# Twelve pairs of gate tiles by seven products, attention pipelined and moved ahead of the convolution, eight modulation columns moved to the down projection

## The chip, the cores and the metric

The kernel runs on one core of a Trainium2 chip. The metric is the device time of one execution, in microseconds (us); several runs are taken and their median is compared. The profile is one execution taken by the hardware profiler, with times counted from its first instruction. Engines are named TensorE (PE in the profile; its weight loads are PEld), VectorE (DVE), ScalarE (ACT), GpSimd (POOL) and SyncE (SP), whose queue issues most of the transfers.

## The reference

One layer of a hybrid diffusion backbone, on 640 tokens: 512 of a sample (a grid 8 by 64) and 128 of a prompt. Everything is float32; the matmuls meet the accuracy by splitting each operand in a high and a low part and adding three products (high x high, high x low, low x high).

```python
def token_mixers(h, lw, ...):
    proj = h @ lw['w_in']
    (a_x, a_b, a_c, b_q, b_ff, b_fb, b_i, b_g, c_q, c_k, c_v, d_u, d_v) = jnp.split(proj, IN_SPLITS, axis=-1)
    y_a = a_b * dwconv3(a_c * a_x, lw['conv_a_w'], lw['conv_a_b'])
    y_b, s_f, s_b = hgrn2_bidir(b_q, b_ff, b_fb, b_i, b_g, ...)
    y_c = ...   # neighbourhood attention (sample), full attention (prompt)
    y_d = chunk_gmlp(d_u, d_v, lw['gmlp_norm_g'], lw['gmlp_ws'], lw['gmlp_b'])
    g_a, g_b, g_c, g_d = jnp.split(jax.nn.sigmoid(h @ lw['w_gate'] + lw['b_gate']), N_BRANCH, axis=-1)
    merged = (g_a * (y_a @ lw['w_br_a']) + g_b * (y_b @ lw['w_br_b'])
              + g_c * (y_c @ lw['w_br_c']) + g_d * (y_d @ lw['w_br_d']))
    return merged @ lw['w_o'], kh, vh, s_f, s_b

def trunk_layer(x, cvec, lw, ...):
    mod = jax.nn.silu(cvec) @ lw['w_ada'] + lw['b_ada']
    sh1, sc1, g1, sh2, sc2, g2 = jnp.split(mod, 6, axis=-1)
    h = rmsnorm(x, lw['norm1_g']) * (1.0 + sc1) + sh1
    mix, ... = token_mixers(h, lw, ...)
    x = x + g1 * mix
    h = rmsnorm(x, lw['norm2_g']) * (1.0 + sc2) + sh2
    x = x + g2 * conv_ffn(h, lw['w_up'], lw['ffn_conv_w'], lw['ffn_conv_b'], lw['w_down'])
```

The model width is 1024, each branch is 256 wide, the gates are 4 x 1024 columns, the feed-forward is 2 x 2816 up and 2816 down.

## The kernel before

The order of the large matmuls is written as a list of units (`units`). After the first part (norm, modulation columns 0 to 15 by matmul, and the first three tiles of the input projection) the units run in this order:

- **Input projection** in thirteen sections of two tiles (`SECTIONS`), h @ w_in. Most are `in_tile`: 128 output features by 640 tokens, 48 matmuls of 128x128 by 320 columns (8 k-steps, three products, two halves of 320 tokens). Sections i and dv are `tok_tile` (tokens on the partitions). `evac_in` takes each tile out of PSUM (pool `psg`, two buffers of two banks).
- **Gates** (`gate_tile`): for branches in the order a, d, b, c, each with 8 tiles of 128 columns. The plain form has 48 matmuls for the gate and 12 for the branch product y @ w_br; ScalarE takes the sigmoid, VectorE multiplies and adds into `merged` (regions MG0, MG1). Branches b and c are computed in `GPAIR` = 8 pairs of tiles (n, n + 4): `g_pair` computes the 2 x 2 block product of a pair with seven block products of 12 matmuls each (`gprod`, L1110) in place of eight, and two branch products of 12 (`g_branch`, L1123). For this it needs sums of weight blocks (`g_sums`) and four new operands from h (`g_operands`, from a copy of h in DRAM, `hdr`), which lie in regions that attention uses (X0, X1, F) and are computed once attention is done.
- **Output projection** (`wo_tile`), norm 2, **up projection** (`up_all`, 22 pairs by seven products), **down projection** (`down_tile`, two halves of 512 columns, 11 steps each, 30 matmuls a step; `down_out` multiplies by g2 and adds the residual).

Beside this stream run generators ("jobs"): `hgrn` (started at the end of section q), `gmlp` (du), `conva` (ab), `attn` (cv), `ada_cols` (q), `g_operands`. Each yields a time, and is taken on by `tick` when the estimated time of the matmuls traced so far (`now`) has passed it; that sets where its matmuls stand between the others. `SLACK` stretches a job's yields, `HD` holds yields. `drain` runs all jobs until a condition holds. The framework then orders each engine's instructions by this order and by what is ready in its own estimate; from the pairs on parts are kept in program order (`Ordered`).

`hgrn` runs seven levels on VectorE with small matmuls between (L533), state updates (L582), and, once section g is done, its outputs (L620 to L627) and transposes (L642). Its helper `along` (L476) multiplies ten blocks by two columns of ones, twice. At its end it splits y_b (region E) and y_d (region D) in high and low parts (`split_y`, L657). `attn` waits for y_d. It works on 16 units (8 windows x 2 heads) in four groups (`GS`); before each group it waits until another gate's sigmoid is traced (`R["sig"]`), then runs scores and exponentials for the group's four units (`s1`), then normalisation and transposes (`s2`, L847) and the value products (`s3`, L864). Its result, yc, is in region C.

`ada_cols` computes the modulation columns 16 to 47, each a 512 KB load into the one buffer H and two VectorE passes over 1024 elements (L248); columns 16 to 23 give g1, 24 to 39 give sh2 and sc2, 40 to 47 give g2. `gain_rows` transposes g1 or g2 and writes it to DRAM (`growd`), `gain_load` reads it back to all partitions (L271).

## Time and profile before

| | |
|---|---|
| median of 3 runs | 1061.43 us (1060.1, 1061.43, 1061.75) |
| profiled execution | 1065.27 us, span 1063.5 us |
| granted TensorE clock, mean | 0.989 |
| PE busy | 1038.6 us (98%), 7696 matmuls |
| DVE busy | 775.0 us (73%) |
| ACT busy | 517.3 us (49%) |
| POOL busy | 118.0 us (11%) |
| bytes moved | 155.05 MB |

A row of a timeline or of the chain gives its start, its length, the engine, the line and the operation, with the tiles written and read; x is the count merged into the row. Merged matmuls overlap, so the distance between the starts of two rows says more than a row's length. A row of stretches gives busy times by engine, the granted clock and the DMA load of each stretch.

### The profile page before, as it was taken

Reading aid. Unit: us, or ns where it says so; the run is one execution under the profiler, and the core shown is the slowest. Engines: PE = TensorE matmul, PEld = TensorE weight load, DVE = VectorE, ACT = ScalarE, POOL = GpSimd, SP = SyncE. Lnnn points to the kernel's source line nnn. Section 1 sums busy time; section 2 is a strip of 40 time slices with the busy share of each in tenths; the row PEclk is TensorE's granted clock in tenths of the full one; section 3 lists DMA queues with packets and bytes.
Section 4 is the critical chain, followed back from the end, with each engine's and each line's share of the span. In section 5 each row is a group of like instructions: output and inputs, shape, how many; then the busy total and the mean of one; then the engine's idle time right before and its main releaser. Section 6 shows DMA issues by size and latency. Waiting matters only on the chain.

```text
span 1063.5 us, 18801 instructions
## 1 busy us (share of the span) xinstructions
PE 1038.6 (98%) x7696; PEld 974.0 (92%) x7696; DVE 775.0 (73%) x1232; ACT 517.3 (49%) x863; POOL 118.0 (11%) x150
## 2 busy tenths in 40 slices
PE   7999999999999999999999998999999999999997
PEld 5699989999999999999998788999999999888886
DVE  6558898853688887676764687998888887745534
ACT  6252253332444422444452387777777667534432
POOL 1013120020011000000010022211221111001101
PEclk9998999999999999999999999999999999999999
DMA  9662334343443452212244258775566667952212
GB/s 373 229 215 88 121 101 139 123 126 112 131 149 110 160 162 85 86 53 97 89 140 159 100 160 167 176 184 144 144 154 163 163 165 208 371 189 78 80 40 100
DMA packets 53431, 155.05 MB, mean 146 GB/s; under 512 B 7745, under 2 KB 16353, under 8 KB 51681
## 3 DMA queue, kind: packets, MB, share of 16 engines
q1 hardware_dynamic: 42128, 130.11, 36.5%
q0 software_dynamic: 11216, 23.74, 10.9%
q8 instruction: 60, 0.98, 0.4%
q14 instruction: 27, 0.21, 0.1%
HBM read 124.44 MB, written 15.49 MB: 132 GB/s over the span
## 4 chain that ended last, share of the span: by engine, by line
PE 86%; DVE 7%; ACT 2%; DMA 2%; issue 2%; POOL 0%; SPq 0%; POOLq 0%; DVEq 0%; ACTq 0%
PE g L382 22%; PE g L1406 20%; PE m L1110 9%; PE g L1714 8%; PE m L1714 6%; PE m L1406 5%; PE g L1123 3%; PE m L1243 2%; PE g L1243 1%; PE g L926 1%; PE g L1816 1%; PE m L213 1%; DVE junk L248 1%; PE m L864 1%; DMA MG<-raw 1%
## 5 line engine op out<-in xcount | busy, mean ns | idle before, releaser
L382 PE MATMUL g<-XH,w 128*128 128x320 f32 x1088 | 258.0, 315 | 0.2
L382 PEld LDWEIGHTS g<-XH,w 128*128 128x128 f32 x1088 | 185.1, 188 | 4.9 <-issue 2.9
L382 PE MATMUL g<-XL,w 128*128 128x320 f32 x544 | 168.2, 309 | 0.0
L382 PEld LDWEIGHTS g<-XL,w 128*128 128x128 f32 x544 | 102.4, 188 | 0.3 <-issue 0.3
L348 DVE TENSOR_TENSOR w<-raw,w 128x1024 fp32r<-128x1024 f32 (+1 forms) x37 | 49.9, 1349 | 24.2 <-ACT w L347 23.5
L248 DVE SCALAR_TENSOR_TENSOR junk<-H,S 128x1024 bf16<-128x1024 f32 x32 | 41.2, 1288 | 19.5 <-DMA H<-in_w_adt_dram 19.4
L335 DVE TENSOR_TENSOR w<-raw,w 128x1024 fp32r<-128x1024 f32 x34 | 44.3, 1302 | 13.5 <-ACT w L334 12.2
L347 ACT ACTIVATE w<-raw 128x1024 fp32r<-128x1024 f32 (+1 forms) x37 | 42.6, 1152 | 20.4 <-PE g L382 10.0
L334 ACT ACTIVATE w<-raw 128x1024 fp32r<-128x1024 f32 x34 | 35.8, 1054 | 31.2 <-PE g L1243 15.8
L1714 PE MATMUL g<-w,XH 128*128 128x512 f32 (+1 forms) x216 | 47.5, 372 | 0.0
L1714 PEld LDWEIGHTS g<-w,XH 128*128 128x128 f32 x216 | 38.5, 188 | 7.3 <-DVE X L133 0.2
L133 DVE SCALAR_TENSOR_TENSOR X<-X,p2t,X 128x641 f32<-128x641 f32 x44 | 38.9, 884 | 2.4 <-ACT X L133 1.5
L133 DVE SCALAR_TENSOR_TENSOR X<-MG,p2t,X 128x641 f32<-128x641 f32 x44 | 38.9, 884 | 2.1 <-ACT X L133 1.2
L248 DVE SCALAR_TENSOR_TENSOR H<-H,S 128x1024 f32<-128x1024 f32 x32 | 39.5, 1236 | 0.6
L1714 PE MATMUL m<-w,XH 128*128 128x512 f32 (+1 forms) x180 | 39.9, 369 | 0.0
L1714 PE MATMUL g<-w,XL 128*128 128x512 f32 (+1 forms) x180 | 39.7, 372 | 0.0
L1406 PE MATMUL g<-XL,C 128*128 128x320 f32 x240 | 38.7, 310 | 0.1
L1406 PE MATMUL g<-XL,w 128*128 128x320 f32 x240 | 38.8, 311 | 0.0
L1714 PEld LDWEIGHTS g<-w,XL 128*128 128x128 f32 x180 | 32.3, 188 | 6.5 <-DVE dt L1725 0.3
L1406 PEld LDWEIGHTS g<-XL,C 128*128 128x128 f32 x240 | 35.9, 188 | 1.0 <-ACT MG L133 0.8
L1406 PEld LDWEIGHTS g<-XL,w 128*128 128x128 f32 x240 | 35.9, 188 | 0.7 <-ACT MG L133 0.3
L1714 PEld LDWEIGHTS m<-w,XH 128*128 128x128 f32 x180 | 31.3, 189 | 5.3
(514 smaller groups left out, 2537.1 us busy)
## 6 DMA issues: line engine op xcount, KB each, us to landing
raw<-in_w_up_dram SPq DMA_DIRECT2D x35, 512.0 KB, 5.1
H<-in_w_adt_dram SPq DMA_DIRECT2D x32, 512.0 KB, 3.5
raw<-in_w_in_dram SPq DMA_DIRECT2D x22, 512.0 KB, 4.0
raw<-in_w_down_dram SPq DMA_DIRECT2D x22, 512.0 KB, 3.6
raw<-in_w_gate_dram SPq DMA_DIRECT2D x16, 640.0 KB, 3.9
raw<-in_w_gp_dram SPq DMA_DIRECT2D x12, 640.0 KB, 3.9
actd<-X POOLq DMA_DIRECT2D x22, 320.5 KB, 5.6
G<-in_w_up_dram SPq DMA_DIRECT2D x11, 512.0 KB, 4.5
```

The costliest lines, as they stand in the source:

```text
L133: r = f(*args, **kw)
L248: vec.scalar_tensor_tensor(raw if v else junk, raw, 1.0, cr[:, v], ALU.mult, ALU.mult, accum_out=ar[:, v:v + 1])
L334: act(w[0], raw, AF.Copy)
L335: vec.tensor_tensor(w[1], raw, w[0].bitcast(F32), ALU.subtract)
L347: act(w[:, 0], raw, AF.Copy)
L348: low = lambda: vec.tensor_tensor(w[:, 1], raw, w[:, 0].bitcast(F32), ALU.subtract)
L382: mm(o, w[:, h, k0 + k, :], r(k)[:, s], start=(k == 0 and i == 0), stop=(k == kt - 1 and i == 2))
L1110: mm(o, w[:, k, :], x[:, k, :], start=(first and k == 0 and j == 0), stop=(k == 3 and j == 2), skip_group_check=True)
L1123: mm(pb[:, c, 0:HC], w[:, h + k, :], y[:, x, k, s], start=(k == 0 and j == 0), stop=(k == 1 and j == 2))
L1243: mm(m, mh[k // 2][:, hx, k % 2, t * P:(t + 1) * P], wo[q][:, hw, k % 2, :], start=(k == 0 and i == 0), stop=(k == 7 and i == 2))
L1406: mm(o, w[:, k, :], x[:, k, :], start=(first and k == 0 and j == 0), stop=(k == 3 and j == 2), skip_group_check=True)
L1714: mm(acc[nh][t + c0 // 256][:, 0:c1 - c0], sl[k][hx][:, t * P:(t + 1) * P], w[:, hw, k, c0:c1], start=(kk_ == 0 and k == 0 and i == 0), st ...
```

## The change

- **Order**: `SECTIONS` becomes ff, fb, q, i, g, dv, du, ck, cq, cv, ac, ax, ab. g stands ahead of dv, attention's sections ahead of the convolution's.
- **Gates**: the branch order becomes d, a, b, c. Only d (8 tiles) stays plain; a, b and c are 12 pairs. `g_operands` starts at the first tile of d. It first writes yc to DRAM (`ycd`), since region C is now used for its operands; yc is read back into region A, by POOL's queue, when branch a's last pair is done. The regions of the pairs' weights and of the split `merged` are changed with it.
- **Attention**: the groups and the wait for sigmoids are gone. `s1` of the next window is issued ahead of `s2` and `s3` of the present one.
- **Convolution**: ac is copied by ScalarE to region MG0; ax and ab are multiplied in as VectorE takes them out of PSUM; `conva` starts after ax and does only the three taps. The first tile of ac drains the jobs until hgrn's outputs are issued; ab's eviction drains them until the taps are.
- **Modulation columns**: 16 to 39 are due 5 instead of 45 after q and pause between hgrn's outputs and its end; 40 to 47 (g2) run in the down projection, with the silu vector loaded again into MG1, and g2 is read into S0 at the last step of the first half.
- **Due times**: `along` yields after each of its ten matmuls and counts 0.22 for each; the slack of hgrn is 1.3 (1.4), of attention 1.1 (1.15).

```diff
-SECTIONS = ["ff", "fb", "q", "i", "dv", "du", "ax", "ac", "ab", "g", "ck", "cq", "cv"]
+SECTIONS = ["ff", "fb", "q", "i", "g", "dv", "du", "ck", "cq", "cv", "ac", "ax", "ab"]
...
-    def ada_cols():
+    def ada_cols(fs, tag="S0"):
...
-        for f in range(16, 48):
+        for f in fs:
+            while "hgrn_out" in R and "hgrn_done" not in R:
+                yield 1
...
+        elif sec in ("ac", "ax", "ab"):
+            if (sec, n) == ("ac", 0):
+                drain(lambda: "hgrn_out" in R)
+            y = need("MG0", "YA", [P, 2, 2, T])
+            if sec == "ac":
+                act(c2(y[:, 0, n]), psv, AF.Copy)
+                return
+            if sec == "ab":
+                drain(lambda: "conv" in R)
+            x = y[:, 0 if sec == "ax" else 1, n]
+            vec.tensor_tensor(c2(x), psv, c2(x), ALU.mult)
+            if (sec, n) == ("ab", 1):
+                R["ya"] = split_y("A", y[:, 1].rearrange("p n t -> p (n t)"))
...
-                pe(0.11)
-                if i % 3 == 2:
-                    yield 0
+                pe(0.22)
+                yield 0.5
...
-        for g, g1 in GS:
-            n0 = R["sig"]
-            while R["sig"] == n0 and g >= AW:
-                yield 0.4
-            for u in range(g, g1, 2):
-                s1(u)
-                yield 2 * HD[2]
-            for u in range(g, g1):
-                s2(u)
-                yield 0.8
-                if u % 2 == 1:
-                    s3(u - 1)
-                    yield 0.8
+        s1(0)
+        yield 2 * HD[2]
+        for u in range(0, 16, 2):
+            if u < 14:
+                s1(u + 2)
+                yield HD[6]
+            for i in range(2):
+                s2(u + i)
+                yield 1.2
+            s3(u)
+            yield HD[8]
...
-                start(ada_cols(), HD[7])
+                start(ada_cols(range(16, 40)), HD[7])
...
-    BR = ["a", "d", "b", "c"]
+    BR = ["d", "a", "b", "c"]
...
-    GPAIR = 8
+    PAIRS = [(bi, n) for bi in range(1, 4) for n in range(4)]
+    GPAIR = len(PAIRS)
+    ycd = dram.tile([P, 2, 2, T], F32, name="ycd")
...
-    MHT = ["E", "D", "B", "A"]
+    MHT = ["E", "A", "B", "D"]
...
-        f = [region(t, [P, 2, 4, HC]) for t in "AB"]
+        nc.sync.dma_start(ycd, R["yc"].bitcast(F32))
+        f = [region(t, [P, 2, 4, HC]) for t in "CB"]
...
-        return region("DBA"[i], [P, 5, 4, P], F32R)
+        return region("CBD"[i], [P, 5, 4, P], F32R)
...
+            if PAIRS[q] == (1, 3):
+                R["yc"] = region("A", [P, 2, 2, T], F32R)
+                pool.dma_start(R["yc"], ycd)
...
-            drain(lambda: "ada" in R)
+            drain(lambda: "ada39" in R)
...
-        grows["g2"] = gain_load(1, "MG1")
+        start(ada_cols(range(40, 48), "MG1"))
...
+        if (nh, kk_) == (0, 10):
+            drain(lambda: "ada47" in R)
+            grows["g2"] = gain_load(1, "S0")
```

## The prediction

> **What bounds the kernel now.** I read the page first (engine totals, then the chain that ended last), then the chain in order of time to find the stage that is rewritten, then the list of what TensorE waited for.

> ```profile
> PE 1038.6 (98%) x7696; PEld 974.0 (92%) x7696; DVE 775.0 (73%) x1232; ACT 517.3 (49%) x863; POOL 118.0 (11%) x150
> PE 86%; DVE 7%; ACT 2%; DMA 2%; issue 2%; POOL 0%; SPq 0%; POOLq 0%; DVEq 0%; ACTq 0%
> 380.44 28.49 PE g L382 x192
> 409.20 28.15 PE g L382 x192
> 437.35 8.80 PE m L1110 x60
> 446.15 1.76 PE g L1123 x12
> 447.91 5.28 PE m L1110 x36
> 453.19 1.76 PE g L1123 x12
> 562.43 1.76 PE g L1123 x12
> ```

> The chain is TensorE's own for 86% of the span: only matmuls removed, waits removed or new waits can move the end. The rows after 380 us give the price. In the plain gate stage 192 matmuls of 320 columns take 28.15 us, 146.6 ns each, one behind the other; a plain tile is 48 for the gate and 12 for the branch, 60 matmuls or 8.80 us. In the pair stage, from 437.35 us, one period is 8.80 + 1.76 + 5.28 = 15.84 us (products and branches of two neighbouring pairs), and the eight pairs end at 564.19 us, with no wait between: 126.84 / 8 = 15.85 us. Two plain tiles cost 17.60 us, a pair 15.84 us.

> ```profile
> 88.00:92.00 4.00, 4.00 (x32) 4.00 (x32) 4.00 (x5) 1.06 (x1) 2.31 (x1) 0.86 0.33 121
> 92.00:96.00 4.00, 2.56 (x12) 2.27 (x12) 4.00 (x5) 1.05 (x2) 1.29 (x1) 0.50 0.00 0
> 96.00:100.00 4.00, 4.00 (x27) 3.80 (x27) 4.00 (x6) 0.77 (x2) 0.00 (x0) 0.78 0.40 131
> 104.00:108.00 4.00, 4.00 (x24) 4.00 (x23) 3.54 (x5) 0.74 (x1) 0.72 (x1) 0.57 0.19 43
> 101.02 0.73 PE L476 MATMUL m<-heads,E 128*128 128x2 f32 x6
> 103.08 0.72 PE L476 MATMUL m<-heads,E 128*128 128x2 f32 x6
> PE m L533 <- issue: 1.2, 1, 1.2
> PE m L680 <- DVE X L685: 0.9, 1, 0.9
> ```

> The first four rows are stretches of the span: length, then busy time of PE, PEld, DVE, ACT and POOL, then the granted clock and DMA. Ahead of the gate stage two things cost TensorE time. Its granted clock falls twice, to 0.50 at 92 to 96 us and 0.57 at 104 to 108 us: 4 x (0.14 + 0.50 + 0.22 + 0.43) = 5.2 us of clock lost; the PE was idle for 1.44 us of the second stretch, which would have cost half of that anyway, so 4.4 us is what a full clock could return. Both falls come right behind the bursts of L476 (`along`), matmuls of two columns, three in a row with three ordinary ones between. And between 148 and 160 us TensorE waits 1.2 + 0.9 = 2.1 us for hgrn and gmlp.

> **Four more pairs (tiles of a).** Removed: 4 pairs x 12 matmuls x 146.6 ns = 7.04 us of TensorE, all on the path. The weights read are the same 2 x 640 KB. What is added lies on VectorE and ScalarE: sums and splits for a pair instead of two plain splits.

> ```profile
> 440.00:560.00 120.00, 120.00 (x819) 119.90 (x819) 87.28 (x128) 57.16 (x99) 2.90 (x5) 1.00 0.32 105
> 120.00:160.00 40.00, 37.63 (x888) 33.94 (x889) 38.28 (x68) 17.66 (x31) 10.22 (x10) 1.00 0.32 100
> ```

> In the pair stage VectorE is busy 87.28 of 120 us and TensorE all 120, so TensorE covers that work: 87.28 / 120 x 15.84 = 11.5 us of VectorE in a pair; were VectorE to wait elsewhere for over 4.3 us of a pair, the excess would show. The later start of the second row block of merged (now region A, held by yc until the last branch matmul) is two copies, hidden by the first 6.8 us step of the output projection. Term: -7.04 us.

> **`along` spread out.** The two-column matmuls now go one at a time with due times 0.5 x 1.3 = 0.65 us apart, so two k-steps of six ordinary matmuls lie between any two. Bounds: 0, if the falls have another cause, and -4.4 us. I take -3.0: both falls follow the bursts, and a second section now behind `i` changes the neighbours, so some of it may stay. Extra changes between the streams are at most 12 of about 0.1 us and lie within that.

> [...]

> **g moved ahead of dv; attention ahead of the convolution.** The same tiles in another order: no matmul more. What moves is when attention may start.

> ```profile
> 185.07 1.05 PE L582 MATMUL m<-E,D 128*128 128x128 f32 x8
> 215.99 1.00 PE L627 MATMUL m<-E,MG 128*128 128x64 f32 x8
> 249.72 1.49 DVE L657 TENSOR_TENSOR E<-MG,E 128x1280 fp32r<-128x1280 f32 x1 [1.34 <-ACT E L656]
> 379.96 0.48 PE L864 MATMUL m<-B 128*64 128x128 f32 x3
> 380.52 1.20 SPq L1011 DMA_DIRECT2D B<-hdr  x2
> 407.24 1.49 DVE L1036 TENSOR_TENSOR F<-B,F 128x1280 fp32r<-128x1280 f32 x1
> hdr<-MG SPq DMA_DIRECT2D x2, 1280.0 KB, 7.0
> ```

> hgrn's last state update is at 186.1 us, but its outputs start at 215.99 us, held by g, and are split at 251.2 us, 35.2 us later. With g early they start near 187 and end near 222 us; cv, now the 14th tile behind q as g was, ends near 223 us. Attention can start there instead of at 268.4 us, where it starts now behind cv. Now it lasts to 380.4 us, 112 us, since each of its four groups waits for a gate's sigmoid; pipelined, by its due times (8 steps of 5.9 x 1.1 us, some 11 us ahead, its own matmuls), some 70 to 80 us. The pairs start at 437.35 - 8 x 8.80 - 3 = 364 us, and need the first new operand after 24 matmuls, at 367.5 us.
> Behind attention come the operands: 380.4 to 408.7 us is 28.3 us, plus yc written out first (a transfer of the same 1280 KB took 7.0 us), 35.3 us. Attention at 223 + 75 ends at 298, operands at 333: 34 us to spare, cost 0. Attention unchanged at 112 us gives 370.3 us, 2.8 us late.
> The convolution: ax and ab leave PSUM through VectorE instead of ScalarE, and ab's first eviction now waits for the taps on VectorE, behind attention's work. There are two accumulators, so ab's second tile (48 x 146.6 ns = 7.04 us) covers it; without the cover it would cost such a tile. Bound 0 to +7.0, taken 0. yc's reload on POOL's queue has 4 pairs (63 us) before its use: 0.

> **The modulation columns.** 24 now start earlier, and pause while hgrn's outputs run; 8 go to the down projection.

> ```profile
> L334 ACT ACTIVATE w<-raw 128x1024 fp32r<-128x1024 f32 x34 | 35.8, 1054 | 31.2 <-PE g L1243 15.8
> L248 DVE SCALAR_TENSOR_TENSOR junk<-H,S x4: 1219/1225/1226, 200.9 to 219.7; 128x1024 bf16<-128x1024 f32 x4
> 275.56 1.20 DVE L248 SCALAR_TENSOR_TENSOR junk<-H,S 128x1024 bf16<-128x1024 f32 x1
> 402.07 1.23 DVE L248 SCALAR_TENSOR_TENSOR junk<-H,S 128x1024 bf16<-128x1024 f32 x1
> 912.34 0.33 SPq L271 DMA_DIRECT2D MG<-growd  x1
> S<-in_cc_dram SPq DMA_DIRECT2D x1, 1024.0 KB, 6.7
> x2d<-X SPq DMA_DIRECT2D x4, 512.0 KB, 2.6
> MG<-growd SPq DMA_DIRECT2D x1, 1024.0 KB, 9.3
> 974.86 0.69 DVE L1725 TENSOR_TENSOR dt<-g,MG 128x512 f32<-128x512 f32 x1
> 932.66 5.44 PE g L1714 x24
> 980.48 4.08 PE m L1714 x18
> 984.56 2.07 PE g L1714 x12
> 942.25 54.86 SPq L358 DMA_DIRECT2D raw<-in_w_down_dram  x9
> 940.00:960.00 20.00, 20.00 (x90) 16.58 (x89) 7.96 (x10) 6.71 (x10) 0.00 (x0) 1.00 0.27 91
> ```

> Now g2 is fetched at 912.34 us, as soon as region MG1 is free, 62 us before its first use. In the new order the silu vector takes that place, and g2 comes last. In the time of the profile: vector at 912.3 + 6.7 = 919.0, silu 2.1 (twice a pass of ScalarE over 1024 columns, 1.05 us), then eight columns at a period p and 2.5 us for the last one's two passes (1.2 each), 923.7 + 7p; rows written 2.6, read back 8.8 (between 6.7 and 9.3, transpose and copy within it): 935.1 + 7p. The second half has three accumulators of its own (18 matmuls from 980.48 us); TensorE needs the first half's back at 984.56, less two mults of 0.69: 983.2 us. A column took 18.8 / 3 = 6.3 us where its loads ran free and 126.5 / 14 = 9.0 us where they stood in SP's queue behind gate weights. p = 6.3 ends at 979.2 (cost 0), 6.87 is the break-even, 9.0 ends at 998.1 (+15). The due times written are 4.4 + 2 x 1.4 = 7.2 us, near one w_down load per step of 30 matmuls (5.44 / 24 x 30 = 6.8 us), which SP's queue now alternates with: 985.5, cost +2.3 us, and that I take. The extra loads also stand in SP's queue ahead of w_down's and of the stored activations; VectorE is idle for 12 of 20 us behind those there, so they are not late, and the eight columns' 20 us fit in.

> **Sum.** 1065.27 us is the profiled execution (span 1063.5 and 1.8 around it), 3.84 above the median 1061.43 of the three runs. -7.04 - 3.0 + 2.3 = -7.7: 1057.5 in that frame, 1053.7 us against the median.

> **Rivals.**
> All waits vanish: p at 6.3, clock full, and the 2.1 us before 160 us gone since gmlp moves away from hgrn: -7.04 - 4.4 - 2.1 = -13.5, 1047.9 us. For it: all these are waits on VectorE or queues that the new order eases; against it: VectorE is at 38.28 of 40 us there already.
> [...]
> Operands late: earlier columns put some three more, 3 x 2.5 us, on that full VectorE, hgrn ends up to 8 us later, and attention is no shorter than now: +2.8 to +10.8 on the forecast, about 1060.5 us. Against it: no sigmoid to wait for.
> Slower than before: the gain g2 comes late in the down projection. At p = 9.0, as in the gate stage where the same loads share SP's queue with weights, TensorE stands 15 us: -10.0 + 15, 1066.4 us. It decides from p = 8.6 on (10.0 + 2.1 us of stall). For it: SP's queue spends 54.86 us on nine loads in this stage, each behind a buffer; against it: a step is 6.8 us and not 8.8.

> **Chances.** Forecast 0.43, all waits vanish 0.18, clock still falls 0.14, operands late 0.12, g2 late 0.13. Some 0.2%, 2.1 us, is what a measurement of this kernel tells from no change. The first three are faster; the fourth is half the same, some of it faster, little slower; the fifth mostly slower: faster 0.79, same 0.08, slower 0.13. The range runs from the best case, 1047, to 1061.5, which takes in most of the late operands and p up to 8.

> **What would show it.** Right: L382 matmuls down by 8 x 60 = 480, L1110 up by 4 x 84 = 336, L1123 by 96, a pair period still 15.84 us; the clock at 1.00 between 85 and 110 us; attention starting near 223 us and last at 310 or before; no PE wait at the first pair; the first L1725 some 2 us late and a short PE wait at the second half's fourth row block. Wrong: a PE wait above 5 us in either place, a clock fall elsewhere, or pairs longer than 16 us.

## The result: no difference, with the pairs' gain spent ahead of them

The changed kernel took 1062.49 us (median of 20 runs) against 1061.38 for the one before (20 runs): a ratio of 1.0001 between the means of the runs, 95% interval 0.9988 to 1.0013 (the two medians alone differ by 0.1%). The forecast was 1053.7 us, and 1062.49 lies above its range. The profiled execution took 1062.54 us with a span of 1060.8, so it is a typical run; the profile of before (1065.27) was 3.9 us above its median, and a second profile of the same kernel (the first experiment) gave a span of 1060.2. I compare with that one where it matters.

The page of the changed kernel, totals and chain:

```profile
PE 1030.6 (97%) x7648; PEld 968.3 (91%) x7648; DVE 795.8 (75%) x1278; ACT 521.0 (49%) x890; POOL 119.3 (11%) x151
PE 91%; DVE 3%; ACT 2%; DMA 2%; issue 1%; POOL 1%; SPq 0%; POOLq 0%; ACTq 0%; DVEq 0%
```

The 48 matmuls are gone (7696 to 7648), and TensorE is the chain even more than before. The chain in order of time, around the gate stage:

```profile
315.00 56.52 PE g L382 x384
371.52 8.80 PE m L1112 x60
380.32 1.76 PE g L1125 x12
382.08 5.28 PE m L1112 x36
559.95 1.76 PE g L1125 x12
```

Twelve pairs take 371.52 to 561.71 us: 190.19 us, 15.85 each, with no wait. Eight pairs and eight plain tiles took 126.84 + 70.4 = 197.24, so the 7.04 us came in full. They were lost ahead of the pairs. Below, the stretch from the first input projection to the first pair is taken as one window in three profiles: before, before again, changed (length, then busy time of PE, PEld, DVE, ACT, POOL, granted clock, DMA).

```profile
59.30:437.35 378.05, 374.06 (x3452) 359.00 (x3453) 278.52 (x468) 140.11 (x232) 38.30 (x33) 0.99 0.39 126
59.80:435.37 375.57, 371.57 (x3452) 356.54 (x3453) 278.49 (x468) 140.14 (x232) 38.21 (x33) 1.00 0.39 127
59.77:371.52 311.75, 302.80 (x2971) 289.91 (x2972) 235.17 (x407) 113.00 (x205) 38.20 (x33) 0.98 0.40 127
```

Less 70.4 us for the eight plain tiles that became pairs, the stretch was 307.65 and 305.17 us before; it is 311.75 now, 6.58 more than in the second profile. TensorE stands idle in it for 311.75 - 302.80 = 8.95 us, before 4.00 in both profiles. Its waits now, and those of before in the second profile:

```profile
PE m L648 <- DVE MG L652: 4.0, 1, 4.0
PE g L924 <- ACT E L928: 2.9, 1, 2.9
PE m L538 <- issue: 1.9, 1, 1.9
```
```profile
PE g L926 <- ACT E L930: 2.3, 1, 2.3
PE m L533 <- issue: 1.5, 1, 1.5
```

The wait for the multiplications of hgrn's output (4.0 us) is new. At each of the three waits of the changed kernel the granted clock falls (a row ends with the clock, the DMA load and GB/s):

```profile
96.00:100.00 4.00, 1.80 (x8) 1.80 (x9) 4.00 (x7) 1.37 (x3) 0.00 (x0) 0.64 0.60 207
100.00:104.00 4.00, 4.00 (x20) 4.00 (x19) 2.59 (x5) 1.51 (x3) 0.00 (x0) 0.51 0.15 20
152.00:156.00 4.00, 2.05 (x85) 1.71 (x84) 4.00 (x7) 0.74 (x1) 1.15 (x1) 0.89 0.17 28
156.00:160.00 4.00, 4.00 (x22) 4.00 (x20) 4.00 (x9) 2.14 (x3) 0.00 (x0) 0.68 0.65 232
224.00:228.00 4.00, 0.98 (x4) 0.96 (x5) 2.45 (x6) 0.00 (x0) 0.00 (x0) 0.85 0.61 189
228.00:232.00 4.00, 4.00 (x23) 3.93 (x23) 3.17 (x9) 0.00 (x0) 0.00 (x0) 0.72 0.00 0
```

Clock lost is a stretch's length times what is missing from 1.00: 4 x (0.36 + 0.49 + 0.11 + 0.32 + 0.15 + 0.28) = 6.84 us. The second profile of before has one fall, 4 x 0.42 = 1.68 us; the first had 5.16:

```profile
148.00:152.00 4.00, 4.00 (x22) 3.65 (x19) 4.00 (x6) 3.84 (x10) 3.82 (x5) 0.58 0.43 127
```

In the changed kernel the clock stood at half already in the last 1.30 us of the waits; 0.65 of the 6.84 us are thus idle time as well, and are counted once here. The account against the second profile: idle +4.95, clock lost while busy +4.51 (6.19 against 1.68), TensorE's busy time at full clock -2.88 (371.57 - 70.4 - 1.68 = 299.49 before, 302.80 - 6.19 = 296.61 now); together +6.58. With the pairs' -7.04 and some +1.1 behind the pairs, whose cause is open, the spans differ by +0.6.

### The profile page after: what moved, and what is told of

Read it like the earlier page. It is cut to its first block, busy times and chain, and to the rows that moved or that the text cites. A ratio compares the mean times of both kernels' runs of the same rounds, so it can differ in the third digit from the quotient of the medians.

```text
span 1060.8 us, 18792 instructions
## 1 busy us (share of the span) xinstructions
PE 1030.6 (97%) x7648; PEld 968.3 (91%) x7648; DVE 795.8 (75%) x1278; ACT 521.0 (49%) x890; POOL 119.3 (11%) x151
## 3 DMA queue, kind: packets, MB, share of 16 engines
q0 software_dynamic: 11360, 25.05, 11.2%
## 4 chain that ended last, share of the span: by engine, by line
PE 91%; DVE 3%; ACT 2%; DMA 2%; issue 1%; POOL 1%; SPq 0%; POOLq 0%; ACTq 0%; DVEq 0%
PE g L1411 20%; PE g L382 19%; PE m L1112 14%; PE g L1722 8%; PE m L1722 6%; PE m L1411 5%; PE g L1125 4%; PE m L1248 3%; PE g L1248 2%; PE g L924 1%; PE g L1824 1%; PE m L538 1%; PE m L211 1%; DMA MG<-raw 1%; PE m L864 1%
## 5 line engine op out<-in xcount | busy, mean ns | idle before, releaser
L382 PE MATMUL g<-XH,w 128*128 128x320 f32 x832 | 205.6, 321 | 0.0
L382 PEld LDWEIGHTS g<-XH,w 128*128 128x128 f32 x832 | 144.9, 191 | 3.8 <-issue 2.4
L382 PE MATMUL g<-XL,w 128*128 128x320 f32 x416 | 130.3, 313 | 0.0
L382 PEld LDWEIGHTS g<-XL,w 128*128 128x128 f32 x416 | 79.7, 192 | 0.2 <-issue 0.2
L335 DVE TENSOR_TENSOR w<-raw,w 128x1024 fp32r<-128x1024 f32 x34 | 41.5, 1221 | 18.0 <-ACT w L334 17.3
L334 ACT ACTIVATE w<-raw 128x1024 fp32r<-128x1024 f32 x34 | 35.8, 1053 | 24.5 <-PE g L1248 16.1
L1112 PE MATMUL m<-XH,w 128*128 128x320 f32 x192 | 45.0, 309 | 0.0
L348 DVE TENSOR_TENSOR w<-raw,w 128x1024 fp32r<-128x1024 f32 (+1 forms) x29 | 41.4, 1426 | 3.9 <-ACT w L347 3.8
L347 ACT ACTIVATE w<-raw 128x1024 fp32r<-128x1024 f32 (+1 forms) x29 | 32.4, 1118 | 17.6 <-issue 6.6
L248 DVE SCALAR_TENSOR_TENSOR junk<-H,S 128x1024 bf16<-128x1024 f32 x24 | 31.4, 1309 | 11.5 <-DMA H<-in_w_adt_dram 11.5
L1411 PE MATMUL g<-XL,w 128*128 128x320 f32 x240 | 38.8, 310 | 0.0
L1411 PEld LDWEIGHTS g<-XL,w 128*128 128x128 f32 x240 | 35.9, 188 | 0.7 <-ACT MG L131 0.3
## 6 DMA issues: line engine op xcount, KB each, us to landing
raw<-in_w_up_dram SPq DMA_DIRECT2D x35, 512.0 KB, 5.1
H<-in_w_adt_dram SPq DMA_DIRECT2D x32, 512.0 KB, 3.5
raw<-in_w_in_dram SPq DMA_DIRECT2D x22, 512.0 KB, 4.4
raw<-in_w_down_dram SPq DMA_DIRECT2D x22, 512.0 KB, 3.6
G<-in_w_up_dram SPq DMA_DIRECT2D x11, 512.0 KB, 4.8
```

The costliest lines, as they stand in the source:

```text
L248: vec.scalar_tensor_tensor(raw if v else junk, raw, 1.0, cr[:, v], ALU.mult, ALU.mult, accum_out=ar[:, v:v + 1])
L334: act(w[0], raw, AF.Copy)
L335: vec.tensor_tensor(w[1], raw, w[0].bitcast(F32), ALU.subtract)
L347: act(w[:, 0], raw, AF.Copy)
L348: low = lambda: vec.tensor_tensor(w[:, 1], raw, w[:, 0].bitcast(F32), ALU.subtract)
L382: mm(o, w[:, h, k0 + k, :], r(k)[:, s], start=(k == 0 and i == 0), stop=(k == kt - 1 and i == 2))
```

## The experiments

Theory A, as first stated: the products pay in full, and VectorE's queue, filled by modulation columns that start 40 us earlier in the kernel's own estimate of time (`now`), makes the waits that eat the gain. Rivals: the gain of the pairs is an accident of one profile (B); the waits come from the order of hgrn and its neighbours, not from the columns (C). Ratios are to the kernel before, measured beside each; the changed kernel's own is 1.0001. An eviction is the copy that takes a finished tile out of PSUM and so gives its buffer back.

**Before, again.** No edit.

> The kernel before, profiled once more; its first profile stood 3.9 us above its own median. Theory A (the products' 7.0 us arrive in full, and the input projections of the changed kernel lose about as much): this profile stands near the median of 1061.4, its first pair starts 3 to 4 us earlier than 437.35, at about 433.5, and TensorE's clock falls less than the 5.2 us that it lost between 80 and 112 in the first profile. Theory B (the first profile was typical in its front, and the products give less than 7.0 in other runs): the first pair starts at 437 again, and the 3.9 us are missing behind it.

Ratio 1.000 (0.998 to 1.002). The span is 1060.2 and the first pair starts at 435.37 us, not 437.35, with 1.68 us of clock lost instead of 5.16: 2 of the 3.9 us lay in the front. The two bursts of `along` are there, and a longer wait for the eviction (2.3 us against 1.4), but no fall between 84 and 112 us: the first profile's falls come in some executions only.

**Eight pairs.**

```
-    PAIRS = [(bi, n) for bi in range(1, 4) for n in range(4)]
+    PAIRS = [(bi, n) for bi in range(2, 4) for n in range(4)]
...
-            if PAIRS[q] == (1, 3):
+            if PAIRS[q] == (2, 0):
```

> The changed kernel with eight pairs instead of twelve: branch a's eight gate tiles are whole again. Theory A: 4 x 12 x 146.6 ns more TensorE work, +7.0 us: 1069.5, the first pair at 371.52 + 4 x 17.6 = 441.9 us. Theory B (the four further pairs pay little or nothing outside one lucky profile): 1062 to 1065.

The second edit moves the reading back of yc behind the first pair that is left. 1.0055 (1.0033 to 1.0077): 0.54% over the changed kernel, 5.7 us; its first pair starts at 439.34 us. Rival B falls. Its own profile lost 3.40 us of clock, the changed kernel's 6.84, so 7.04 and the difference agree within what the front varies.

**Columns held back.**

```
-            while "hgrn_out" in R and "hgrn_done" not in R:
+            while "tots" in R and "hgrn_done" not in R:
```

> The changed kernel, its modulation columns held back from the end of hgrn's seven levels (173 us) to the end of hgrn, and not only from its output on. Theory A: the 4.0 us wait of hgrn's transposes for the multiplications of VectorE at 223 goes, with most of the clock's fall behind it (4 x 0.15 + 4 x 0.28 = 1.7 us): 1062.5 - 5.7 = 1056.8. Theory C (VectorE's queue there is full anyway, by the weights' low parts and the normalisation that waits 3.4 us for GpSimd): the wait shrinks by one column's 1.2 to 2.5 us at most: 1060 to 1062. If the columns only move their waits elsewhere: 1062.5.

1.0011 (0.9993 to 1.0029): nothing. The wait is 4.4 us. The trace shows why: passes of columns still run on VectorE between 207 and 229 us. Whether they were traced before the hold or put forward by the framework's ordering, the trace does not say; the hold did not keep them out of the queue.

**`along` in bursts again, in the changed kernel.**

```
-                pe(0.22)
-                yield 0.5
+                pe(0.11)
+                if i % 3 == 2:
+                    yield 0
```

> The changed kernel with the two-column matmuls of hgrn three at a time again, as before the change. If the bursts bring the clock's falls: granted clock under 0.9 in the stretches right behind the bursts, 3 to 4.4 us lost, 1066. [...]

1.0095 (1.0065 to 1.0124), some 10 us more, a median of 1072.34 us and well over the 1066 expected. First pair at 382.72, 11.2 us later. Idle time 12.22 us (8.95), clock lost while busy 10.28 (6.19), busy time at full clock 300.36 (296.61): each gives about a third. The bursts themselves cost about 4 us; the rest is a front whose waits are longer (4.5 us for the multiplications, 1.9 for the state updates).

**Without the early columns.** This leaves out the loads and passes of columns 16 to 39; a constant stands for each result.

```
+            if f < 40:
+                yield HD[4]
+                ar = sp.tile([P, 2], F32, tag="red", name=nm("ar"))
+                vec.memset(ar, 0.5)
+                ...
+                continue
             raw = region("H", [P, D])
```

> The changed kernel without the work of modulation columns 16 to 39: their loads and VectorE's passes of 2 x 1.22 us each are left out, a constant stands for each result. Theory A (VectorE's in-order queue, filled by columns that start 40 us earlier than before, makes the new waits): both TensorE waits go, 4.0 us for the multiplications of hgrn's output and 2.9 us for an eviction of section i, and the clock's falls behind them (about 3.4 and 1.7 us): first pair at 371.5 - 12 = 359.5 us, time 1050.5. Theory C (the waits come from the order of g and hgrn and from VectorE's other work): under 2 us gained, 1061 to 1062.5.

0.9983 (0.9965 to 1.0001), under 2 us. The waits of this kernel (its lines are 13 further down):

```profile
PE g L937 <- ACT E L941: 3.1, 1, 3.1
PE g L395 <- ACT gt L978: 2.6, 1, 2.6
PE m L551 <- issue: 1.3, 1, 1.3
```

The 4.0 us wait is gone, so the columns do make it. The eviction's wait is not theirs (3.1), another of 2.6 us has come, and 8.52 us of clock are lost. Theory A is half right at best: one wait is the columns', and removing it alone pays nothing that can be measured.

**Columns started later.** The start goes from 5 to 36. A start later than 36 was not tried: by the kernel's text the columns would then still need the regions H and S0 when the pairs take them.

```
-HD = [4, 5, 2.1, 7, 4.4, 1.4, 1.5, 5, 2.0, 2, 11]
+HD = [4, 5, 2.1, 7, 4.4, 1.4, 1.5, 36, 2.0, 2, 11]
```

> The changed kernel with the columns started 36 instead of 5 of the kernel's own clock after section q (before: 45). Theory A: the first column's passes come at about 105 us, so the 2.9 us wait at 95 us goes with the clock's fall behind it (3.4 us); the 4.0 us wait at 223 stays: 1062.5 - 6.3 = 1056.2. If the wait only moves with the columns into hgrn's levels (TensorE waiting for evictions or keys between 110 and 170 us): 1061 to 1063.

1.0025 (1.0003 to 1.0047), a miss. The waits stay, 3.0 and 4.1 us: the wait for the eviction does not need the columns. The profiled run took 1059.95 us, the median is 1065.93; what the other runs lost I cannot see.

**The kernel before with `along` spread alone.** The opposite of the edit above.

> The kernel before with one part of the change alone: the two-column matmuls of hgrn one at a time, 0.5 apart. By the busy time of TensorE between the first input projection and the first pair, less waits and less lost clock (300.2 us before in its second profile, 296.1 in the changed kernel, 300.2 with the bursts put back), the bursts cost about 4 us themselves, and the clock's falls behind them 0 to 5 us more: 1062 - 4 to -6 = 1056 to 1058. If the 9.8 us of the run with bursts put back belong to the bursts alone: 1052. If bursts lie in TensorE's shadow in the kernel before: 1061 to 1062.

1.0082 (1.0062 to 1.0102), about 9 us slower where I expected 4 to 6 faster. Its waits, and the window from the first projection to the first pair:

```profile
PE m L641 <- DVE MG L645: 5.5, 1, 5.5
PE g L925 <- ACT E L929: 3.2, 1, 3.2
59.52:446.56 387.04, 376.80 (x3452) 361.49 (x3453) 278.84 (x468) 140.32 (x232) 40.84 (x33) 0.98 0.39 123
```

This is the run that overturned the columns' start as the whole cause: the two longest waits of the changed kernel arise in the kernel before, with its columns where they were, from the later due times alone (the second `along` ends at 118.9 us, in the second profile of before at 103.5). Columns do stand in the way: ahead of the multiplications VectorE has two low parts, a column, and another that waits 2.83 us for its load. Idle time goes from 4.00 to 10.24 us, clock lost from 1.68 to 8.56, and TensorE's busy time at full clock stays the same (299.38 against 299.49, both less the 70.4). In the changed kernel the same spreading was worth some 10 us, here it costs 9: its sign depends on what it moves hgrn against.

**Transposes later.**

```
-HD = [4, 5, 2.1, 7, 4.4, 1.4, 1.5, 5, 2.0, 2, 11]
+HD = [4, 5, 2.1, 7, 4.4, 1.4, 1.5, 5, 2.0, 2, 17]
```

> The changed kernel with the transposes of hgrn's output placed 6 x 1.3 = 7.8 us later in TensorE's order. Theory A (the transposes find the multiplications queued behind a column's pass that waits for its load, and behind a weight's low part): the multiplications run at 226.6 us anyway, the transposes now come at 229, the 4.0 us wait goes with the fall behind it: 1062.5 - 5.7 = 1056.8. If VectorE's order follows the transposes (another column and low part slip in between): the wait stays, 1062 to 1063.

1.006 (1.0035 to 1.0085), slower. The wait for the multiplications stays at 3.6 us, and one of 3.6 for a gate's sigmoid is new: VectorE's order follows the transposes. Here, too, moving work in time only exchanged waits.

**Three tiles.** So I took away what makes the engines wait, at fixed times. VectorE and the transposes in the changed kernel (timeline, PE and then DVE rows, without the rows under 0.3 us):

```profile
222.63 0.27 PE L648 MATMUL m<-cst,MG 128*128 128x128 f32 x1
227.02 0.47 PE L648 MATMUL m<-cst,MG 128*128 128x128 f32 x1 [3.97 <-DVE MG L652]
```
```profile
215.59 2.02 DVE L643 TENSOR_TENSOR MG<-MG,hss 128x1280 f32<-128x1280 f32 x1 [3.42 <-POOL hss L277]
217.54 1.76 DVE L348 TENSOR_TENSOR w<-raw,w 128x1024 fp32r<-128x1024 f32 x1
219.35 1.21 DVE L248 SCALAR_TENSOR_TENSOR junk<-H,S 128x1024 bf16<-128x1024 f32 x1
220.60 1.23 DVE L248 SCALAR_TENSOR_TENSOR H<-H,S 128x1024 f32<-128x1024 f32 x1
222.07 1.22 DVE L348 TENSOR_TENSOR w<-raw,w 128x1024 fp32r<-128x1024 f32 x1
225.35 1.23 DVE L248 SCALAR_TENSOR_TENSOR junk<-H,S 128x1024 bf16<-128x1024 f32 x1 [2.06 <-DMA H<-in_w_adt_dram]
226.62 1.75 DVE L652 SCALAR_TENSOR_TENSOR MG<-m,p1t,MG 128x128 f32<-128x128 f32 x5
```

Between the normalisation (L643) and the first multiplication (L652) stand two low parts of weights (L348), a column (two passes, L248), and half of the next, which waits 2.06 us for its load. TensorE has made the transpose of 222.63 us, but its multiplication runs only at 226.62. TensorE stands: there are four PSUM tiles of this kind, and it needs one back. Three tiles hold all ten transposes.

```
-        for t in range(5):
+        for ts in ((0, 1), (2, 3), (4,)):
             m = pm()
...   (all transposes of ts into m, then all multiplications)
```

> The changed kernel, the transposes of hgrn's output written to three PSUM tiles (two token tiles in each) in place of five, of four that there are; VectorE's order stays as it is. Theory A' (VectorE's queue holds two low parts and a pass and a half of the columns between the normalisation and the multiplications, and TensorE stands because the fourth transpose needs a PSUM tile back): TensorE's 4.0 us wait goes and the clock's fall behind it, 1.7 us: 1062.5 - 5.7 = 1056.8, first pair at 365.8. If the wait moves to the attention's PSUM tiles right behind: 1061 to 1062.5. If the clock falls without an idle stretch as well: 1058.5.

0.9976 (0.9957 to 0.9996). The wait for L652 is gone, another has come at the attention's first transposes; this profile lost the same 6.84 us of clock:

```profile
PE m L749 <- ACT G L458: 3.1, 1, 3.1
```

They read section cv, whose eviction stands on ScalarE behind the split of hgrn's output (229.15 us), which has waited 9.43 us for the same multiplications. VectorE's queue is the cause of both, and the first wait had covered the second.

**Keys on GpSimd.** The other wait, in the changed kernel (PE, ACT, DVE):

```profile
98.20 0.58 PE L924 MATMUL g<-w,XH 128*128 128x256 f32 x1 [2.85 <-ACT E L928]
96.78 0.83 ACT L510 ACTIVATE D<-B 128x640 f32<-128x640 f32 x1 [5.69 <-DVE B L558]
97.48 0.67 ACT L928 ACTIVATE E<-g 128x256 f32<-128x256 f32 x2
95.87 0.81 DVE L558 TENSOR_TENSOR B<-B,A 128x640 f32<-128x640 f32 x1
```

ScalarE is free from 91.1 us on, but the next on its queue is a copy of hgrn's keys (an operand of its next level) that waits 5.69 us for VectorE; the eviction behind it had its data some 5 us before.

```
-            act(klv[:, :, 1, :], blk(kk[:, 1], B)[:, :, 1, :], AF.Copy)
+            if l == 1:
+                pool.tensor_copy(klv[:, :, 1, :], blk(kk[:, 1], B)[:, :, 1, :])
+            else:
+                act(klv[:, :, 1, :], blk(kk[:, 1], B)[:, :, 1, :], AF.Copy)
```

> The changed kernel with one copy of hgrn's keys (the one for its second level, 0.83 us) on GpSimd in place of ScalarE. Theory A' (TensorE's 2.9 us wait at 95 us is for an eviction that stands on ScalarE behind that copy, which itself waits 5.7 us for VectorE): the wait goes and the clock's fall behind it, 4 x (0.36 + 0.49) = 3.4 us: 1062.5 - 6.3 = 1056.2, first pair at 365.2. If the fall belongs to the two-column matmuls ahead of it and not to the wait: 1059.6. If the levels then wait for GpSimd, whose copy of 320 x 2 columns takes 1.7 us: 1061 to 1063.

0.9966 (0.9947 to 0.9986). The wait and its fall are gone; a wait of 2.0 us for a level's update has come at 128 us, with 6.8 us at half clock behind it, so half of the 6.3 arrived (first pair at 368.45, 3.1 earlier).

**Both edits.**

> Both edits together in the changed kernel. Theory A': 1062.5 - 5.7 - 6.3 = 1050.5, first pair at 359.5. If what is gained at one place is lost at the next, as in the run without the columns: 1059 to 1062.

0.9931 (0.9906 to 0.9956), 1056.15 us: clear of the kernel before, and of the changed one by its own ratio. First pair at 364.91. What is left in the front:

```profile
PE m L752 <- ACT G L458: 2.9, 1, 2.9
PE m L541 <- DVE C L561: 2.0, 1, 2.0
58.20:364.91 306.71, 300.71 (x2971) 288.17 (x2972) 235.86 (x408) 112.32 (x204) 40.06 (x34) 0.98 0.41 129
```

**Both edits in the kernel before.**

> Both edits in the kernel before. It has no wait for the multiplications, so the first edit is worth nothing there; the eviction's wait is 1.4 to 2.3 us, with 0 to 5 us of lost clock: 1061.5 - 2 to -5 = 1056.5 to 1059.5. If theory A' holds, the changed kernel with both is then 6 to 9 us under this one; if the products' gain is an accident of one profile, the two are equal.

0.9989 (0.9969 to 1.0009): they are worth nothing measurable there. With both edits on both sides the change is worth 0.9931 / 0.9989 = 0.9942, or 6.2 us (by the two intervals, about 3 to 9).

Four more, on what was left in that version (edits added to the three tiles and the keys).

**Attention 4 later**, `start(starts[sec](), 5.5 if sec == "cv" else 1.5, SLACK[sec])`:

> The changed kernel with the three tiles and the keys' copy on GpSimd, and the attention started 4 of the kernel's clock later. Theory A' (the wait that three tiles moved to the attention's first transposes is the same queue: VectorE's multiplications, then the split's copy on ScalarE, then the eviction of section cv): the 2.9 us wait goes with the clock's fall behind it (1.7): 1056.2 - 4.6 = 1051.6. If it moves on again, to the next that reads the late sections: 1055 to 1057.

0.9973 (0.9954 to 0.9992). The wait went from the first to a later transpose of the attention (1.8 us, for VectorE's copies): it moved on again.

**Levels 2 later as well**, `HD[0]` from 4 to 6:

> The same, with hgrn's levels started 2 x 1.3 = 2.6 us later in TensorE's order. Theory A': the 2.0 us wait of a level's matmuls for VectorE at 128 us goes with the clock's fall behind it (3.4): 5.4 us under the run with the attention later alone, 1046. If VectorE paces the levels (an update of four operations for every level, columns and low parts between), the wait comes back at a later level: 0 to 2 us.

0.9957 (0.9936 to 0.9977). The level's wait shrank from 1.7 to 0.3 us, the attention's grew to 2.7. Neither beats the two edits.

**Eight pairs**, the same edit as above:

> The changed kernel with the three tiles and the keys' copy on GpSimd, but eight pairs instead of twelve. The front is the same, so the pairs alone differ: 1056.2 + 4 x 12 x 0.1466 = 1063.2. If the pairs pay less in the times than in the trace: 1060 to 1061.

1.0030 (1.0006 to 1.0054), about 10 us over the version with twelve; the single times spread from 1059.9 to 1069.9. In the profiles the stretch ahead of the pairs is the same, 434.40 - 57.65 - 70.4 = 306.35 against 306.71 us, and the pairs differ by 7.04. That they pay is settled; by how much in the times is not: the medians differ by over 9 us, the two profiled spans (1058.7 and 1054.4) by only 4.3.

**Bursts**, the same edit as above:

> The changed kernel with the three tiles and the keys' copy on GpSimd, but the two-column matmuls of hgrn in bursts of three again. If the bursts cost what TensorE's busy time says (300.2 against 296.1 us): 1056.2 + 4.1 = 1060.3 and up to 4 us more with falls of the clock behind the bursts. If the 9.8 us of the earlier run with bursts were waits that these two edits take away: 1056 to 1058.

1.0077 (1.0049 to 1.0105), 13 to 16 us over. The waits:

```profile
PE m L761 <- DVE X L757: 4.8, 1, 4.8
PE m L542 <- issue: 2.8, 1, 2.8
57.84:377.37 319.53, 308.91 (x2971) 293.48 (x2972) 235.67 (x408) 112.05 (x204) 38.57 (x34) 0.97 0.39 124
```

Idle 10.62 us and 10.24 us of lost clock, of which 0.70 lie in the waits: 308.91 - 9.54 = 299.37 busy at full clock against 300.71 - 5.01 = 295.70 spread. The bursts cost 3.7 us of busy time; the rest is again another order with other waits.

## Why the prediction was wrong, step by step

- **Four more pairs, -7.04**: right in the trace to 0.01 us, with no VectorE wait in a pair.
- **`along` spread, -3.0**: what it removes was read right, what it moves was missed. Of eight bursts that ran unbroken at full clock in the five profiles with bursts, four ended in a fall, with TensorE busy throughout; of the 13 profiles with the two-column matmuls spread none shows a fall without a wait that began at most 4 us before it. One of the four, in the kernel before with both edits (first and last group of the burst, then 1 us windows):

```profile
95.78 0.73 PE L476 MATMUL m<-heads,E 128*128 128x2 f32 x6
98.86 0.30 PE L476 MATMUL m<-heads,E 128*128 128x2 f32 x2
98.00:99.00 1.00, 1.00 (x10) 1.00 (x11) 1.00 (x3) 0.33 (x1) 0.00 (x0) 0.99 0.00 0
99.00:100.00 1.00, 1.00 (x7) 1.00 (x6) 1.00 (x2) 0.00 (x0) 0.34 (x1) 0.50 0.17 45
102.00:103.00 1.00, 1.00 (x9) 1.00 (x9) 0.81 (x2) 0.00 (x0) 0.00 (x0) 0.81 0.02 8
```

  The burst lasts 3.4 us, and the clock is at 0.50 from its end on. (Each of the three matmuls in a row is recorded as two, so the rows have x6.) Besides, spreading saves some 3.7 us of busy time at full clock in the changed kernel, with and without the two edits, but nothing measurable in the kernel before. I priced its side effect at nothing: hgrn then comes later against everything else. Alone in the kernel before that cost about 9 us, and in the changed kernel the falls behind waits took the place of those behind bursts.
- **The step that failed: what is moved, 0.** I followed TensorE's order and the attention's start, and bounded only operands and convolution. The real price lay in the order of the queues: hgrn's multiplications behind low parts and columns on VectorE (TensorE idle for 3.97 us), an eviction behind a copy on ScalarE (2.85 us). Idle time +4.95 and clock lost while busy +4.51 us, which with 2.88 us of busy time saved make +6.58 in place of -3.0. In the rivals I had VectorE at 38.28 of 40 us, and used it for the attention's operands, not for TensorE's transposes. That the pause (`hgrn_out` to `hgrn_done`) keeps columns out of hgrn's output I took as written; the trace has passes of columns there at 219 to 227 us.
- **Attention, operands, convolution, 0**: right. Attention runs from 233.6 to 315.0 us (I had 223 to 298), the low part of the third new operand ends at 344.9 (333), 12 us late but ahead of the pairs, and no pair waits.
- **g2, +2.3**: 0 in the changed kernel. A column takes 5.9 to 8.2 us (p of 7.2 was the guess), g2 is there at 978.62 against the needed 983.2 (980.7 in this run's time, whose pairs end 2.5 us earlier), and TensorE does not wait:

```profile
966.44 1.23 DVE L248 SCALAR_TENSOR_TENSOR junk<-H,MG 128x1024 bf16<-128x1024 f32 x1 [0.54 <-DMA H<-in_w_adt_dram]
972.98 0.38 SPq L271 DMA_DIRECT2D S<-growd  x1
978.62 0.69 DVE L1733 TENSOR_TENSOR dt<-g,S 128x512 f32<-128x512 f32 x1 [6.11 <-DMA S<-growd]
```

  I had overlooked another place: the transposes of the last columns stand in TensorE's order. Ten of the experiments with the late columns wait there, for 0.2 to 2.6 us (2.6 in the run with the columns held back).
- **The frame**: I took 3.84 us off for the median and 3.0 for `along`. The second profile, nearer the median, has only 1.68 us of lost clock, none of it behind the bursts: about half of the 3.84 (2.0 us) lay ahead of the pairs, in the very falls that the 3.0 counted again.
- **The clock.** In the traces it is 1.00 or 0.50, and in each of the 18 profiles all its changes between 56 us and the first pair lie on one grid of marks 3.41 us apart (in the changed kernel at 97.10, 103.93, 155.13, 158.55, 226.81 and 230.23 us). Four of the eight bursts ended in a fall, so I was right not to set the term to 0; but the changed kernel's falls all stand at a wait (2.85, 1.95 and 3.97 us), and for these the forecast had no term.
- **What the marks show.** In these profiles a wait went with a fall by the part of it that lay in one window, the 3.41 us between two marks. Below, the 2.3 us wait of the second profile of before is cut by a mark into 1.35 and 0.97 us and brings no fall; the 1.95 us wait of the changed kernel lies within one window and brings one. Ahead of the pairs, in all 18 profiles, each of the 23 windows at full clock with 1.85 us or more of idle time ended in a fall, and of those with less than 0.8 us only the four with a burst; between these values both happen: the 3.6 us wait of the run with the transposes later is cut into 1.84 and 1.73 us and brings none, the 1.76 us of the eviction's wait that lie ahead of the mark at 97.10 us in the changed kernel bring one. The bursts follow the same marks: the four that brought a fall left 0.17 to 0.28 us of their window to other matmuls, the four that did not 0.53 to 0.86 us. So whether a burst or a short wait cost anything in these runs was in part chance, that of where the marks lay in an execution.

```profile
90.58:93.99 3.41, 2.06 (x17) 1.86 (x16) 3.41 (x5) 0.13 (x1) 1.52 (x2) 1.00 0.00 0
93.99:97.40 3.41, 2.44 (x20) 2.44 (x21) 3.41 (x4) 1.30 (x3) 0.40 (x1) 1.00 0.13 16
```
```profile
151.72:155.13 3.41, 1.46 (x83) 1.14 (x83) 3.41 (x6) 0.74 (x1) 1.16 (x1) 1.00 0.02 5
155.13:158.54 3.41, 3.41 (x20) 3.38 (x14) 3.41 (x8) 0.70 (x1) 0.00 (x0) 0.50 0.59 171
```

What stays open: no run has the new order of the sections alone, so how the loss is shared between the order, the due times of `along` and the earlier columns is not shown beyond the runs above; nor why the medians of two experiments (columns later, eight pairs with both edits) lie 5 to 6 us above their own profiled runs.

## What to carry to other kernels

When steps of a pipeline are moved, write out the order of each engine's queue at the places where TensorE needs it back, and ask what stands ahead of that one instruction (here a copy that waited 5.69 us, ahead of an eviction whose data had been there for some 5 us); busy shares over 40 us do not show it. Delays did not pay for such stalls here, they exchanged them for others; what paid was to give the waiting engine a buffer, and to take the blocking instruction off the shared queue. And profile the kernel before twice: what one execution lost to the clock (5.16 us here), the next may not lose (1.68 us), and then it can't be gained.
